# HGRN score products of a head issued by block width, both scan directions together, in place of tile by tile

## The chip, the cores and the metric

One NeuronCore of a Trainium2 chip runs the kernel. The metric is the device time of one execution in microseconds (us); three runs of the kernel before are shown, and one more execution was taken with a profile. The engines are TensorE (PE, with its weight loads as PEld), VectorE (DVE), ScalarE (ACT), GpSimd (POOL) and SyncE (SP); transfers are issued by the queues of SP and POOL.

## What is computed

The reference is a model of two layers on 256 context and 512 latent tokens of width 1024: the first layer mixes by retention and windowed attention, the second by a gated linear recurrence (HGRN) in both directions; after each comes a mixture of 32 experts. The change is in the second layer's mixer. Cut to that:

```python
def hgrn2_scan(q, k, v, log_f, s0):                 # 8 heads, dk = dv = 128, chunks of C = 16
    def step(s, inp):
        qn, kn, vn, fn = inp
        a = jnp.cumsum(fn, axis=2)
        o_inter = jnp.einsum('bhcd,bhde->bhce', qn * jnp.exp(a), s)
        diff = a[:, :, :, None, :] - a[:, :, None, :, :]
        dec = jnp.exp(jnp.where(lower, diff, NEG_INF))
        scores = jnp.einsum('bhid,bhjd,bhijd->bhij', qn, kn, dec)
        o_intra = jnp.einsum('bhij,bhje->bhie', scores, vn)
        a_last = a[:, :, -1:, :]
        s_new = jnp.exp(a_last[:, :, 0, :])[..., None] * s + jnp.einsum('bhjd,bhje->bhde', kn * jnp.exp(a_last - a), vn)
        return s_new, o_inter + o_intra
# forward and backward over the context, then over the latents from the context's final states; the two are added
```

## The kernel before

The method `odd` (L1178) runs a loop over eight heads. For each it splits the head's weights into two half-precision parts (`wsh`, `wsl`), projects all tokens (PSUM tiles `px`), and makes from them the gates `sig`, the output gate `gs` and the queries `q`; then it calls `hgrn` (L1281). The kernel works with chunks of 128 tokens in place of 16. Per head and direction d (0 forward, 1 backward) `hgrn` takes the logarithm of the gates (`lf`, L1286), their running sums (`a`, L1290 and L1291), the decayed keys `kp` (L1302) and queries `qp`, and the operands of the scores.

The scores of a tile of 128 tokens are not one product, because the exponents need a reference point near both tokens. `eq` and `ek` hold, per direction, 1024 columns: 512 with a reference in each block of 32 tokens, 256 for the off-diagonal parts of blocks of 64 (halves of 32), and 256 for those of blocks of 128 (halves of 64). The operands of the first kind are finished by L1333 and L1334, those of the two others by L1340 and L1341, eight operations in all. On PE, for each direction and each of the four latent tiles t, one full 128x128 product is written into the PSUM tile `hs`, then a 64x64 product over its off-diagonal quarter, then two 32x32 products over the smaller off-diagonal parts. Stationary operands are 128, 64 and 32 columns wide; the narrow ones stand at a column position of the array equal to the partition where their output begins. A matmul in float32 shows as two records in the trace.

When a direction's 16 products are done, VectorE applies its triangular mask (`am`, L1358). Then come the transposes of `kp` (`ktp`, L1366), their copies `kt`, the products `u`, the states `S` (L1376), and after both directions the output `ho`, its mean square `hms` and the gated output `y`. After the last head, `mix_out` multiplies `y` by the output weights (`po`), routes the tokens, and `moe` streams the experts' weights (`mw`) through rings of buffers while PE computes `pa` and `ya` (64 columns wide) and `pb` and `yb` (32 wide).

The code is written for one engine queue each; a planner of the framework puts each engine's instructions into an order of its own when the kernel is built, by their dependencies, their place in the code and its estimates of time. So work of the next head (`px`) and of the same head (`u`) stands between products that are neighbours in the code. PSUM tiles with the tag "s" (`hs`, `hms`) share two buffers; `eq`, `ek`, `a`, `qp` and the pair `lf`/`kp` have one buffer each, `sig` and `q` two.

Of the kernel before, what the change touches and what calls it, by code (L numbers as in the profile page):

```python
# [8 lines left out]
F32 = mybir.dt.float32  # L9
# [73 lines left out]
class Kern:  # L83
# [1197 lines left out]
    def hgrn(s, h, q, sg, gs, v, y, lb, wk, ps, last):  # L1281
        nc = s.nc
        V = nc.vector
        R2 = range(2)
# [26 lines left out]
        eq = wk.tile([128, 2, 1024], F32, name="eq")  # L1311
        ek = wk.tile([128, 2, 1024], F32, name="ek")
# [5 lines left out]
        for d in R2:  # L1318
# [3 lines left out]
            for i, n in enumerate((64, 128)):  # L1322
# [4 lines left out]
                c = slice(512 + 256 * i, 768 + 256 * i)  # L1327
# [7 lines left out]
        for d in R2:  # L1335
            for i, n in enumerate((64, 128)):
                hn = n // 2
                qs, ks, rr = sides(d, n)
                c = slice(512 + 256 * i, 768 + 256 * i)
                V.tensor_tensor(v3(eq[:, d, c], hn), v3(eq[:, d, c], hn), v3(q, n)[:, :, qs], op=ALU.mult)  # L1340
                V.tensor_tensor(v3(ek[:, d, c], hn), v3(ek[:, d, c], hn), v3(kl[:, d], n)[:, :, ks], op=ALU.mult)  # L1341
        ams, Ss = [], []
        for d in R2:
            sp = ps.tile([128, 512], F32, tag="s", name="hs")
            for t in range(4):
                c = slice(t * 128, (t + 1) * 128)
                s.mm(sp[:, c], ek[:, d, c], eq[:, d, c], True, True)
                c64 = slice(768 + t * 64, 832 + t * 64)
                kr, qr = (0, 64) if d == 0 else (64, 0)
                s.mm(sp[kr:kr + 64, t * 128 + qr:t * 128 + qr + 64], ek[:, d, c64], eq[:, d, c64], True, True)  # L1350
                for u in R2:
                    c32 = slice(512 + t * 64 + u * 32, 544 + t * 64 + u * 32)
                    kr, qr = (64 * u, 64 * u + 32) if d == 0 else (64 * u + 32, 64 * u)
                    nc.tensor.matmul(sp[kr:kr + 32, t * 128 + qr:t * 128 + qr + 32], ek[:, d, c32], eq[:, d, c32],
                                     start=True, stop=True, tile_position=(0, kr))
            am = wk.tile([128, 4, 128], F32, tag="am", name="am", bufs=2)
            mask = s.C["ltri" if d == 0 else "utri"]
            V.tensor_tensor(am, v3(sp, 128), mask[:, None, :].to_broadcast([128, 4, 128]), op=ALU.mult)  # L1358

            order = (0, 1, 2, 3, 4, 5) if d == 0 else (1, 0, 5, 4, 3, 2)  # L1360
            kt = wk.tile([128, 5, 128], F32, name="kt", bufs=1)
            for i0, m in ((0, 4), (4, 1)):
                tp = ps.tile([128, 512], F32, tag="t", name="ktp")
                for i in range(i0, i0 + m):
                    t = order[i]
                    nc.tensor.transpose(tp[:, (i - i0) * 128:(i - i0 + 1) * 128], kp[:, d, t * 128:(t + 1) * 128], s.ident)  # L1366
                s.copy(kt[:, i0:i0 + m], v3(tp[:, :m * 128], 128))
            S = wk.tile([128, 5, 128], F32, name="S", bufs=2)
            for i in range(5):
                t = order[i]  # L1370
                u = ps.tile([128, 512], F32, tag="t", name="u")[:, :128]
                s.mm(u, kt[:, i], v[:, t, h * 128:(h + 1) * 128], True, True)
                if i == 0:
                    V.tensor_copy(S[:, 0], u)
                else:
                    V.scalar_tensor_tensor(S[:, i], S[:, i - 1], ge[:, d, t:t + 1], u, op0=ALU.mult, op1=ALU.add)  # L1376
            ams.append(am)
            Ss.append(S)
# [3 lines left out]
        for t in range(4):  # L1382
            c = slice(t * 128, (t + 1) * 128)
# [77 lines left out]
```

## Time and profile before

| | |
|---|---|
| median of three runs | 2120.47 us (2116.13 to 2121.76) |
| the profiled execution | 2118.22 us |
| its span, first to last instruction | 2116.4 us |
| mean granted clock of PE | 0.962 |
| PE, DVE, ACT, POOL busy | 86%, 41%, 27%, 17% of the span |
| score products in the trace (`hs`) | 256 records at L144, 256 at L1354, from 1169.7 to 1485.4 us |

A share of busy time is a mean over stages that have different limits. The stretch from about 1160 to 1485 us, the loop over heads, is where the changed lines run; after 1562 us the kernel streams the second layer's experts. A full granted clock (1.00) is 2.4 GHz, 0.50 is 1.2 GHz.

### The profile page before, as it was taken

The numbers are of one execution on the slowest core, as the hardware profiler recorded it, in microseconds if no ns is written. First come the engines' busy times: TensorE is split into PE (matmuls) and PEld (weight loads), VectorE is DVE, ScalarE is ACT, GpSimd is POOL, SyncE is SP. The second block draws the span as 40 slices with busy tenths as digits, with TensorE's granted clock in tenths as the row PEclk, the third lists the DMA queues.
The fourth block names the chain that finished last, engine by engine and source line by source line (L and its number), as shares of the span: only waits on it lengthen the run. The fifth ranks groups of instructions, "written<-read, shape, count | busy, mean of one in ns | idle before, by whom it ended". The sixth has DMA issues, their size and how long they took to land. (4 is left out here: it accounts for less than half of the span.)

```text
span 2116.4 us, 26460 instructions
## 1 busy us (share of the span) xinstructions
PE 1826.7 (86%) x10109; PEld 856.4 (40%) x10109; DVE 869.3 (41%) x1823; ACT 563.1 (27%) x929; POOL 352.4 (17%) x400
## 2 busy tenths in 40 slices
PE   5999999996989999888589999999949888888872
PEld 2554444453333333233244665565523333333320
DVE  5486455686111111111555766776752112111213
ACT  4355366411111111110334435653201000000000
POOL 2000000013222232211220000000132232222213
PEclk9999999997999999999789999999969999999996
DMA  9525545484999999999853120110459999999996
GB/s 319 194 68 205 210 156 192 185 308 182 410 371 399 410 412 410 410 413 386 295 159 100 41 60 24 60 61 20 162 195 410 411 410 410 410 411 410 410 399 231
DMA packets 168717, 567.73 MB, mean 268 GB/s; under 512 B 21701, under 2 KB 69310, under 8 KB 130658
## 3 DMA queue, kind: packets, MB, share of 16 engines
q1 hardware_dynamic: 145632, 523.88, 64.2%
q0 software_dynamic: 22640, 41.30, 5.5%
q8 instruction: 127, 2.08, 0.4%
q14 instruction: 44, 0.36, 0.0%
q10 hardware_dynamic: 274, 0.10, 0.0%
HBM read 554.59 MB, written 39.91 MB: 281 GB/s over the span
## 5 line engine op out<-in xcount | busy, mean ns | idle before, releaser
L144 PE MATMUL pa<-mw,xa 128*64 128x512 f32 x2048 | 535.4, 606 | 30.6 <-DMA mw<-in_moe_w 26.5
L144 PE MATMUL ya<-mw,gT 128*64 128x512 f32 x1024 | 285.2, 602 | 2.2 <-DMA mw<-in_moe_w 1.2
L144 PEld LDWEIGHTS pa<-mw,xa 128*64 128x64 f32 x2048 | 158.0, 138 | 283.9 <-issue 276.7
L144 PE MATMUL px<-hTh,wsh 128*128 128x512 f16 (+1 forms) x672 | 225.5, 336 | 7.5 <-DVE t L438 2.8
L144 PE MATMUL px<-hTl,wsh 128*128 128x512 f16 (+1 forms) x672 | 225.5, 336 | 1.9 <-DVE hTl L348 1.8
L144 PE MATMUL px<-hTh,wsl 128*128 128x512 f16 (+1 forms) x672 | 225.4, 336 | 0.0
L144 PEld LDWEIGHTS <-wsh 128*128 128x128 f16 x1344 | 130.4, 98 | 117.4 <-issue 19.0
L1027 DVE TENSOR_TENSOR gg<-gg,pa 128x256 f32<-128x256 f32 x64 | 26.9, 420 | 333.0 <-ACT gg L1026 333.0
L937 POOL DMA_INDIRECT yd<-sb,ixm x64 | 65.9, 1029 | 581.0 <-DVE sb L1062 294.1
L144 PEld LDWEIGHTS ya<-mw,gT 128*64 128x64 f32 x1024 | 79.7, 136 | 114.3 <-issue 99.3
L1027 DVE TENSOR_TENSOR gg<-gg,pb 128x128 f32<-128x128 f32 x64 | 18.4, 288 | 253.1 <-ACT gg L1026 253.1
L1026 ACT ACTIVATE gg<-pa 128x256 f32<-128x256 f32 x64 | 24.6, 384 | 361.6 <-PE pa L144 361.6
L138 DVE SCALAR_TENSOR_TENSOR wsl<-w,wsh 128x2048 f16<-128x2048 f32 x34 | 77.8, 2290 | 35.2 <-ACT wsh L135 31.3
L1026 ACT ACTIVATE gg<-pb 128x128 f32<-128x128 f32 x64 | 17.8, 277 | 276.1 <-PE pb L144 276.1
L1032 PE MATMUL gt<-cca,gg 128*128 128x128 f32 x192 | 46.5, 306 | 50.5 <-DVE gg L1027 50.5
L144 PEld LDWEIGHTS <-wsl 128*128 128x128 f16 x672 | 65.9, 98 | 50.2 <-issue 3.9
L927 POOL DMA_INDIRECT hga<-h2d,ixm x64 | 66.7, 1042 | 103.7 <-PE xt L987 77.7
L1032 PEld LDWEIGHTS gt<-cca,gg 128*128 128x128 f32 x192 | 21.5, 141 | 147.5 <-DVE gg L1027 98.8
L144 PE MATMUL adaps<-adaw,cT 128*32 128x512 f32 x384 | 75.8, 636 | 4.2 <-DMA adaw<-in_ada_w 2.9
L937 POOL DMA_INDIRECT yd<-sa,ixm x64 | 64.2, 1004 | 69.5 <-ACT sa L1046 34.1
L992 ACT ACTIVATE xa<-xt 128x512 f32<-128x512 f32 x64 | 38.2, 597 | 140.1 <-PE xt L987 137.8
L144 PE MATMUL pv<-wsh,hTh 128*128 128x512 f16 (+1 forms) x192 | 70.0, 365 | 5.9 <-ACT hTh L1227 5.9
(391 smaller groups left out, 2810.2 us busy)
## 6 DMA issues: line engine op xcount, KB each, us to landing
mw<-in_moe_w SPq DMA_DIRECT2D x384, 1024.0 KB, 20.9
adaw<-in_ada_w SPq DMA_DIRECT2D x40, 1024.0 KB, 5.0
w<-in_od_w_in SPq DMA_DIRECT2D x32, 512.0 KB, 5.5
adaw<-in_ada_w SPq DMA_DIRECT2D x16, 512.0 KB, 7.3
w<-in_ev_w_in SPq DMA_DIRECT2D x8, 1024.0 KB, 7.1
cy<-yd SPq DMA_DIRECT2D x12, 512.0 KB, 9.5
xmid<-oxr POOLq DMA_DIRECT2D x10, 512.0 KB, 6.4
h2d<-ohp POOLq DMA_DIRECT2D x10, 512.0 KB, 3.1
```

The lines of the kernel that those rows point to most:

```text
L138: i = s.nc.vector.scalar_tensor_tensor(lo, v, WS, hi, op0=ALU.mult, op1=ALU.subtract)
L144: return s.nc.tensor.matmul(ps, lhsT, rhs, start=first, stop=last)
L927: i = nc.gpsimd.indirect_dma_start(out=hg[e % NG][g], out_offset=None, in_=hv[g], in_offset=bass.IndirectOffsetOnAxis(ap=cols[g][0], axis= ...
L937: i = nc.gpsimd.indirect_dma_start(out=yv[g], out_offset=bass.IndirectOffsetOnAxis(ap=cols[g][1], axis=0), in_=yt, in_offset=None, bounds_ ...
L992: nc.scalar.activation(x, v, AF.Copy)
L1026: nc.scalar.activation(g[:, c0:c0 + n], p[:, :n], AF.Silu)
L1027: nc.vector.tensor_tensor(g[:, c0:c0 + n], g[:, c0:c0 + n], p[:, n:2 * n], op=ALU.mult)
L1032: nc.tensor.transpose(t[:, c * 128:(c + 1) * 128], g[:, c * 128:(c + 1) * 128], s.ident)
```

## The change

The two PSUM tiles of a head are taken at once, and the 32 matmuls of its scores are issued in three runs: the eight full products, one direction after the other; then the eight 64-wide ones, tile by tile with the direction innermost; then the sixteen 32-wide ones, by tile, block and direction. The masks and all that follows come after, direction by direction as before. The matmuls, their operands and their outputs are the same ones.

```diff
         ams, Ss = [], []
+
+        sps = [ps.tile([128, 512], F32, tag="s", name="hs") for d in R2]
         for d in R2:
-            sp = ps.tile([128, 512], F32, tag="s", name="hs")
             for t in range(4):
                 c = slice(t * 128, (t + 1) * 128)
-                s.mm(sp[:, c], ek[:, d, c], eq[:, d, c], True, True)
+                s.mm(sps[d][:, c], ek[:, d, c], eq[:, d, c], True, True)
+        for t in range(4):
+            for d in R2:
                 c64 = slice(768 + t * 64, 832 + t * 64)
                 kr, qr = (0, 64) if d == 0 else (64, 0)
-                s.mm(sp[kr:kr + 64, t * 128 + qr:t * 128 + qr + 64], ek[:, d, c64], eq[:, d, c64], True, True)
-                for u in R2:
+                s.mm(sps[d][kr:kr + 64, t * 128 + qr:t * 128 + qr + 64], ek[:, d, c64], eq[:, d, c64], True, True)
+        for t in range(4):
+            for u in R2:
+                for d in R2:
                     c32 = slice(512 + t * 64 + u * 32, 544 + t * 64 + u * 32)
                     kr, qr = (64 * u, 64 * u + 32) if d == 0 else (64 * u + 32, 64 * u)
-                    nc.tensor.matmul(sp[kr:kr + 32, t * 128 + qr:t * 128 + qr + 32], ek[:, d, c32], eq[:, d, c32],
+                    nc.tensor.matmul(sps[d][kr:kr + 32, t * 128 + qr:t * 128 + qr + 32], ek[:, d, c32], eq[:, d, c32],
                                      start=True, stop=True, tile_position=(0, kr))
+        for d in R2:
+            sp = sps[d]
             am = wk.tile([128, 4, 128], F32, tag="am", name="am", bufs=2)
```

## Rows read from the trace of the kernel before

**Rows 1.** The page: PE's busy tenths and granted clock, 40 slices of the span.
```profile
PE   5999999996989999888589999999949888888872
PEclk9999999997999999999789999999969999999996
```
**Rows 2.** Stretches of a head: us, busy of each engine, clock; sum of seven.
```profile
core 0: us, PE busy (x) PEld busy (x) DVE busy (x) ACT busy (x) POOL busy (x), PEclk, DMA share, GB/s
1205.00:1244.00 39.00, 37.12 (x250) 23.96 (x250) 30.64 (x48) 18.85 (x22) 0.00 (x0) 1.00 0.30 82
...
sum 311.50, PE 297.35 PEld 186.42 DVE 219.61 ACT 153.94 POOL 1.13; mean PE 42.48 PEld 26.63 DVE 31.37 ACT 21.99 POOL 0.16
```
**Rows 3.** PE's waits, 1155 to 1470 us: us in total, times, longest.
```profile
PE ktp L1366 <- DVE kp L1302: 13.8, 8, 2.9
```
**Rows 4.** Timeline of VectorE, first head: start, us, operation, idle before and releaser.
```profile
1173.75 0.69 DVE L1358 TENSOR_TENSOR am<-hs,ccb 128x512 f32<-128x512 f32 x1 [2.00 <-PE hs L1354]
...
1177.42 0.69 DVE L1358 TENSOR_TENSOR am<-hs,ccb 128x512 f32<-128x512 f32 x1 [2.27 <-PE hs L1354]
```
**Rows 5.** Timeline of SP's queue, and a stretch (as rows 2) of the experts.
```profile
1562.65 72.10 SPq L951 DMA_DIRECT2D mw<-in_moe_w  x32
...
1700.00:1800.00 100.00, 87.90 (x405) 31.23 (x407) 19.83 (x42) 8.81 (x21) 27.50 (x27) 1.00 1.02 410
```
**Rows 6.** Timeline of PE, first head (matmul records; neighbours at one line merged).
```profile
1170.60 0.33 PE L144 MATMUL hs<-eq,ek 128*64 128x64 f32 x2
1170.86 0.26 PE L1354 MATMUL hs<-eq,ek 128*32 128x32 f32 x4
1171.05 0.75 PE L144 MATMUL hs<-eq,ek 128*128 128x128 f32 x4
1171.72 0.26 PE L1354 MATMUL hs<-eq,ek 128*32 128x32 f32 x4
...
1173.63 0.71 PE L144 MATMUL u<-ov,kt 128*128 128x128 f32 x4
...
1182.10 0.39 PE L144 MATMUL ho<-qp,S 128*128 128x128 f32 x2
1182.32 0.39 PE L144 MATMUL ho<-am,ov 128*128 128x128 f32 x2
```
**Rows 7.** Timeline of PE, experts of the first layer, narrow stationary operands.
```profile
931.80 3.74 PE L144 MATMUL pb<-mw,xb 128*32 128x256 f32 x64
935.47 0.65 PE L144 MATMUL pa<-mw,xa 128*64 128x512 f32 x2
...
975.07 1.94 PE L144 MATMUL ya<-mw,gT 128*64 128x512 f32 x8
976.94 0.44 PE L1032 MATMUL gt<-cca,gg 128*128 128x128 f32 x2
```
**Rows 8.** Timeline of PE, windows 1170.861 to 1170.866, then 1170.868 to 1170.869.
```profile
1170.86 0.22 PE L1354 MATMUL hs<-eq,ek 128*32 128x32 f32 x1
...
1170.86 0.22 PE L1354 MATMUL hs<-eq,ek 128*32 128x32 f32 x2
```
**Rows 9.** Timeline of VectorE, second head: the operands of the scores.
```profile
1211.39 1.23 DVE L1333 TENSOR_TENSOR eq<-eq,q 128x1024 f32<-128x1024 f32 x1
1212.53 0.43 DVE L1340 TENSOR_TENSOR eq<-eq,q 128x256 f32<-128x256 f32 x1
...
1214.87 0.43 DVE L1341 TENSOR_TENSOR ek<-ek,sig 128x256 f32<-128x256 f32 x1
```
**Rows 10.** The last head: a stretch (as rows 2), and the timeline of PE.
```profile
1475.70:1489.30 13.60, 13.55 (x77) 10.47 (x77) 3.81 (x10) 1.43 (x2) 0.00 (x0) 0.50 0.01 2
...
1474.01 0.71 PE L144 MATMUL hs<-eq,ek 128*128 128x128 f32 x4 [0.90 <-DVE eq L1333]
1477.31 1.20 PE L144 MATMUL hs<-eq,ek 128*128 128x128 f32 x4
1478.69 1.20 PE L144 MATMUL hs<-eq,ek 128*128 128x128 f32 x4
...
1485.33 0.80 PE L144 MATMUL ho<-am,ov 128*128 128x128 f32 x2
```

## Prediction

> **What bounds the kernel now.** I read the page first, then the stretch in which the changed lines run, then what ends last in that stretch. The page [rows 1] shows TensorE (PE) busy for 86% of the span, at full clock nearly throughout. The score products lie between about 1170 and 1485 us [rows 6, 10], in the loop over eight heads. Cut from one head's first transpose to the next, seven heads take 311.5 us, 44.5 each; PE is busy 297.4 of these, VectorE 219.6, ScalarE 153.9 [rows 2]. The waits of PE say what the rest is: 13.8 us in eight waits for `kp` (L1302), one at each head's beginning, and nothing else of size [rows 3]. So this stretch is bound by PE's instruction stream, with one short wait a head on a chain of VectorE and ScalarE. That chain starts with the Ln of L1286, which needs the next head's gates (`sig`, made from `px` that PE issues behind this head's scores) and the buffer that this head's last `ktp` frees: both are behind the scores on PE, so time taken out of the scores moves the chain too. VectorE stands still for the scores: it waits 2.00 and 2.27 us for them before the two masks of one head [rows 4].
>
> After the loop everything hangs on it: the output projection, the routing, and the experts' weights, whose steady loading begins at 1562.65 us and then runs at 410 GB/s [rows 5]. The loading starts when the routing is done, so what the loop gains moves the end by as much.
>
> **What the scores cost.** One head is shown in [rows 6]. A tile's group is a 128-wide product, a 64-wide and two 32-wide ones (each matmul is two records of the trace). From 1170.86 to 1171.72 a group takes 0.86 us. The 64-wide pair takes 0.26 of it (1170.60 to 1170.86), the four 32-wide records 0.19 (1170.86 to 1171.05), the 128-wide pair the other 0.41. Eight groups: 6.88 us a head, seven heads 48, and the last head more (below).
>
> Most of that isn't work. Products of the same 128 columns that follow each other at one width (`ho`) take 0.22 us a pair, 0.112 a record [rows 6]. By columns, 64 need 0.056 and 32 need 0.028 a record. So of the 128-wide pair 0.19 us is overhead (0.41 - 0.22), of the 64-wide pair 0.15 (0.26 - 0.11), of the 32-wide records, which run two at a time, 0.13 (0.185 - 2 x 0.028): 0.47 us a group is spent on entering and leaving widths, 3.8 us a head.
>
> **The change part by part.**
> *Widths entered.* 24 stages a head become three, so the 0.47 us is paid once. The 128-wide stage then costs 8 x 0.223 = 1.79 us.
> *The narrow stages.* The 64-wide stage has 16 records; with d innermost, neighbours go to different halves of the columns (0 and 64). The 32-wide stage has 32 records, whose neighbours go to 0, 32, 64, 96. Whether they run side by side is read from the experts: 64 records of `pb`, 32 wide with 256 columns, take 3.67 us, 0.057 each where 0.223 would be a single one's; eight of `ya`, 64 wide with 512 columns, take 1.87 us, 0.23 each against 0.45 [rows 7]. So four run together, and two. Lower bounds: 16 x 0.056 / 2 = 0.45 and 32 x 0.028 / 4 = 0.22 us. Upper bounds: no row shows records following each other for long faster than `pb`'s 0.057; at that pace they cost 0.9 and 1.8. I take the lower ones, as the pieces of the present groups already start together: two windows 6 ns apart hold one and two started 32-wide records [rows 8].
> Sum a head: 1.79 + 0.45 + 0.22 + 0.47 = 2.93 us, 3.95 less than now; by the upper bounds 4.96, 1.9 less.
> *A wait that is added.* Both directions' narrow stages now stand ahead of everything else, and alternate. The 64-wide stage needs the last of the eight products of L1340/L1341; in the second head these run from 1212.53 to 1215.3 [rows 9], while the 128-wide stage, beginning as L1333 ends at about 1212.7, ends near 1214.6. That is up to 0.8 us. Up to the last head PE has no wait for these operands that shows [rows 3], so the planner puts other work into such gaps; I charge less than half, 0.35 us. Queued behind that wait on PE are `ktp`, `u`, `ho` and the next `px`. It leaves **3.6 us a head**, 25.2 for seven.
> *The masks.* The second now runs 3.7 us behind the first [rows 4]; both will be released together, where all scores end. `ho` needs both, 1.4 us of VectorE, during which PE has `ktp`, `u` and `px`. If that cover were gone it would cost 0.7 us a head. PSUM has two buffers of this tag and both were in use before; nothing is charged. The number of matmuls, bytes and queue entries stays; SP's and POOL's queues hold nothing of it.
> *The last head* runs at half clock from 1475.7 to 1489.3 [rows 10]: its groups take 1.39 us (1477.31 to 1478.69), and scores with one `u` between stretch from 1474.01 to 1485.33. With the change: 1.9 us for the first stage, a wait for the last L1341 to about 1476.7 (2.6 us behind L1333's end, as in [rows 9]), then the two narrow stages and overhead at 1.39/0.86 of their time, (0.45 + 0.22 + 0.47) x 1.6 = 1.8: the end is near 1478.6, 6.2 us earlier once the `u` pair is left out. But if the half clock lasts as long, the `ktp`, `u` and `ho` that come behind it run at half clock for some 6 us more than now and give about half back. I take 3.5, bounds 2 and 6.2.
> *Sum.* 25.2 + 3.5 = 28.7 us. The profiled execution took 2118.2 us; it would take 2089.5. It lies 2.3 us under the median of the three runs shown (2120.47); I put the forecast between, at 2091.
>
> **The rivals.**
> *Issue is the limit.* The narrow stages go no faster than `pb`'s records: 1.9 us a head, 7 x 1.9 + 2 = 15 us, **2104**. For it: no longer run in the trace is faster. Against: [rows 8], and that `pb` is at its full fourfold rate by columns, so it shows no limit of issue. The Trainium skill, "TensorE: Matmul & The Clock Gate", section "Wait — 56ns, not 53.3ns?", says that start-to-start never drops below about 25 ns however small a matmul is. By that page the 32-wide stage would take 32 x 0.025 = 0.8 us instead of 0.22, an estimate that gives 4.6 us of the gain back: 2096. The two windows [rows 8] disagree for two records on different columns; no row shows a longer run.
> *The planner splits the stages.* It already puts `u` between two scores [rows 6]. Each product of full width inside a narrow stage costs a leaving and an entering, about 0.3 us; six a head would halve the gain: **2105**. Against: PE's other work has room before and behind.
> *The two directions don't overlap.* They write two PSUM banks, and `pb` and `ya` write one. If each change of bank cost what a change of width does, the 64-wide stage would take 8 x 0.26 = 2.1 us, the 32-wide one 16 x 0.185 = 3.0, the first 1.98: 7.1 against 6.9, nothing gained: **2121**.
> *The clock falls* (the slower side). In the last head, soon after a wait of 0.90 us ahead of the scores, PE was granted 0.50 for 13.6 us [rows 10]. Denser scores that end sooner leave PE with more waiting or narrow work in each head. A fall costs half of 13.6, 6.8 us, where PE is the bound; it decides from the fifth of seven heads on (5 x 6.8 = 34, over 28.7). All seven: 2118 - 29 + 48 = **2139** with the median's offset. Against: a wait of 2.9 us for `kp` [rows 3] leaves the clock of the seven other heads at 1.00 (one of their seven rows stands in [rows 2]).
>
> **How the numbers follow.** Forecast 0.68 (2081 to 2100); issue 0.13; split stages 0.06; no overlap 0.05; clock 0.05; something else without effect 0.03. Low end: 7 x 3.95 + 6.2 = 33.9 off 2118.2, and 3 for waits for `kp` that shift: 2081. High end: 15 off the median is 2105, plus the same 3: **2081 to 2108** also holds the issue and split cases. About 0.3%, 6.4 us, is what a measurement of this kernel tells from no change; faster by more 0.87, within 0.08, slower 0.05.
>
> **What would show it.** Right: each head's scores as one 128-wide run of 16 records, one of 64, one of 32, over in 3 to 3.6 us in place of about 7; VectorE's two masks back to back; heads of about 41 us with PE still waiting only for `kp`; the steady load of the experts 29 us earlier; the rest of the trace shifted and otherwise the same. Wrong: 32-wide records 25 or 57 ns apart (issue), `px` or `u` between narrow records (planner), 0.26 us for each 64-wide pair (banks), half clock in other heads, or PE waiting for something new and long between the scores and the next Ln.

## The result and the profile after

The changed kernel takes 2089.33 us (median, 2086.97 to 2089.85), the kernel before 2121.11 in the same measurement: a ratio of 0.9847, 95% interval 0.9828 to 0.9865. It is faster by 31.8 us where 29.5 were forecast (2120.47 to 2091), and 2089.33 lies within 2 us of the forecast. How it came there differs in three terms of the sum, which partly cancel; that is what the rest is about.

The page of the changed kernel, PE's busy tenths and granted clock in 40 slices, to be read against [rows 1]:
```profile
PE   5999999996989999888589999999959888888882
PEclk9999999998999999999889999999969999999996
```
As a whole it is the picture of before: the change isn't to be seen at this size.

The stretches of a head in the changed kernel, cut where PE's wait ahead of the head's first `ktp` begins, columns as in [rows 2]:
```profile
core 0: us, PE busy (x) PEld busy (x) DVE busy (x) ACT busy (x) POOL busy (x), PEclk, DMA share, GB/s
1158.00:1202.90 44.90, 42.64 (x290) 26.26 (x289) 31.23 (x52) 25.54 (x28) 0.00 (x0) 0.96 0.09 24
1202.90:1237.80 34.90, 33.79 (x248) 22.58 (x247) 30.92 (x50) 19.08 (x23) 0.00 (x0) 1.00 0.34 91
...
1325.60:1362.00 36.40, 33.60 (x231) 21.81 (x230) 30.48 (x52) 20.61 (x24) 0.00 (x0) 0.95 0.16 58
...
sum 288.90, PE 277.13 PEld 177.28 DVE 216.99 ACT 153.82 POOL 1.14; mean PE 39.59 PEld 25.33 DVE 31.00 ACT 21.97 POOL 0.16
```
The sum of [rows 2] starts further ahead, 2.5 us before the first `ktp`. Cut as here, the kernel before has:
```profile
sum 310.20, PE 296.93 PEld 186.36 DVE 218.31 ACT 153.54 POOL 1.13; mean PE 42.42 PEld 26.62 DVE 31.19 ACT 21.93 POOL 0.16
```
PE's busy time fell by 19.8 us, and the stretches by 21.3; VectorE, ScalarE and the number of instructions stayed. PE is still the bound, and it still waits for one thing only. PE's waits in these heads (us in total, times, longest), against [rows 3]:
```profile
PE ktp L1373 <- DVE kp L1302: 12.4, 8, 2.8
```
One head's scores before are shown in [rows 6]. PE's timeline of the first and the second head of the changed kernel (start, us, engine, line, operation, records; neighbours at one line are merged, so x32 at L144 holds 16 records of 128 columns and 16 of 64):
```profile
1171.91 2.67 PE L144 MATMUL hs<-eq,ek 128*128 128x128 f32 x32
1174.51 0.46 PE L1359 MATMUL hs<-eq,ek 128*32 128x32 f32 x32
1174.90 0.71 PE L144 MATMUL u<-ov,kt 128*128 128x128 f32 x4
...
1211.63 2.56 PE L144 MATMUL hs<-eq,ek 128*128 128x128 f32 x24
1214.12 0.31 PE L1359 MATMUL hs<-eq,ek 128*32 128x32 f32 x6
1214.36 0.68 PE L144 MATMUL hs<-eq,ek 128*64 128x64 f32 x8
1214.97 0.45 PE L1359 MATMUL hs<-eq,ek 128*32 128x32 f32 x26
1215.34 0.49 PE L144 MATMUL u<-ov,kt 128*128 128x128 f32 x2
```
In the first head the three stages are whole, as the source writes them: from 1171.91 to the start of `u` at 1174.90 they take 2.99 us. In the second the 64-wide stage is in two pieces: eight records of one direction, six 32-wide ones, eight 64-wide ones of the other direction, the other 26. That takes 3.71 us (1211.63 to 1215.34). Seven of the eight heads have this cut. VectorE's timeline in this head shows the last operands of the scores, those of the second direction's 64-wide products:
```profile
1213.35 0.43 DVE L1340 TENSOR_TENSOR eq<-eq,q 128x256 f32<-128x256 f32 x1
1213.68 0.43 DVE L1341 TENSOR_TENSOR ek<-ek,sig 128x256 f32<-128x256 f32 x1
```
They are ready at 1214.11; the 64-wide stage begins at 1213.51, with the other direction.

VectorE's masks of the first head, against [rows 4]:
```profile
1175.03 0.69 DVE L1365 TENSOR_TENSOR am<-hs,ccb 128x512 f32<-128x512 f32 x1 [1.11 <-PE hs L1359]
1175.89 0.69 DVE L1365 TENSOR_TENSOR am<-hs,ccb 128x512 f32<-128x512 f32 x1
```
They follow each other, with one wait for the scores instead of two. The last head, PE's timeline, against [rows 10]:
```profile
1447.86 0.55 PE L1373 MATMUL ktp<-cca,kp 128*128 128x128 f32 x3 [0.93 <-DVE kp L1302]
1454.10 2.66 PE L144 MATMUL hs<-eq,ek 128*128 128x128 f32 x24 [0.91 <-DVE eq L1333]
...
1458.05 0.49 PE L144 MATMUL u<-ov,kt 128*128 128x128 f32 x2
```
A stretch of it, columns as in [rows 2]:
```profile
1454.00:1460.00 6.00, 5.80 (x79) 5.22 (x79) 5.23 (x15) 0.10 (x1) 0.00 (x0) 1.00 0.00 0
```
The start of the experts' steady load on SP's queue, against [rows 5]:
```profile
1534.61 103.61 SPq L951 DMA_DIRECT2D mw<-in_moe_w  x44
```
The scores take 3.95 us (1454.10 to 1458.05) instead of 11.3, and the clock is at 1.00 where it was at 0.50. The load begins at 1534.61 instead of 1562.65: 28.0 us earlier, nearly the whole difference of the two spans (2116.4 to 2088.1).

**Where the time went.** Before, the first `ktp` of the first and of the last head start at 1159.54 and 1468.44 us, after at 1160.27 and 1447.86. The span is 28.3 us shorter: 0.7 lost ahead of the loop, 21.3 won in seven heads, 7.8 from the last head to the end. Of the 21.3, the scores won 19.7 (45.6 to 25.9), PE's idle time 1.5 (the fourth head's wait for `kp` is 1.20 us instead of 2.87), `u`, `ho` and `po` 2.5; `px` and `ktp` lost 1.9 and 0.6, as two stretches of 3.4 us at half clock now lie mostly in them (below).

The same quantities of every profiled execution; the experiments named here follow. All times in us; the scores are PE's time from the first to the last of them without other work between, and "at 0.50" counts the stretches at half clock in the eight heads (one more, of 34 to 38 us, lies around the start of the load in every execution).
```
kernel                     seven heads  last head   scores of      wait    at 0.50
                           ktp to ktp   to load     7 heads/last   for kp
before                       308.9        94.2       45.6 / 10.8    13.8   last head, 13.6
after                        287.6        86.75      25.9 / 3.95    12.4   2 x 3.4
e0 after again               287.8        86.7       25.9 / 3.95    12.4   2 x 3.4
e1 directions apart          295.2        87.2       28.8 / 4.14    15.7   3 x 3.4
e4 wide operands first       281.5        85.95      21.1 / 3.12    12.4   1 x 3.4
e6 32-wide stage first       282.3        86.0       22.1 / 3.29    12.4   1 x 3.4
e3 no alternation            289.95       87.3       25.6 / 3.60    16.0   3 x 3.4
e5 order pinned              283.5        86.1       22.1 / 3.22    14.4   1 x 3.4
e7 last head by tile         284.9        93.8       26.0 / 9.38    12.4   last head, 10.2
e8 before, wide operands     312.5        93.45      46.2 / 9.4     13.7   2 x 3.4; last head, 10.2
```
The first `ktp` starts at 1156.5 us in e3 and at 1163.3 in e0, although the source ahead of the loop is the same. A whole execution can thus differ by some us for reasons that lie ahead of the loop, so the loop's own time is given beside the medians. The experiments were measured in two groups, each beside the kernel before: e0, e1, e4 and e6 (where it took 2119.71 us), and e3, e5, e7 and e8 (2120.08). Between the groups the ratios are compared.

### The profile page after: what moved, and what is told of

It reads as the page before. It is cut to its first block, busy times and chain, and to the rows that moved or that the text cites. A ratio compares the mean times of both kernels' runs of the same rounds, so it can differ in the third digit from the quotient of the medians.

```text
span 2088.1 us, 26462 instructions
## 1 busy us (share of the span) xinstructions
PE 1802.3 (86%) x10109; PEld 843.4 (40%) x10109; DVE 869.0 (42%) x1823; ACT 563.3 (27%) x929; POOL 353.3 (17%) x400
## 5 line engine op out<-in xcount | busy, mean ns | idle before, releaser
L144 PE MATMUL pa<-mw,xa 128*64 128x512 f32 x2048 | 537.0, 608 | 28.9 <-DMA mw<-in_moe_w 24.6
L144 PE MATMUL ya<-mw,gT 128*64 128x512 f32 x1024 | 283.8, 602 | 2.3 <-DMA mw<-in_moe_w 1.5
L144 PEld LDWEIGHTS pa<-mw,xa 128*64 128x64 f32 x2048 | 158.4, 139 | 284.1 <-issue 277.4
L144 PE MATMUL px<-hTh,wsh 128*128 128x512 f16 (+1 forms) x672 | 227.1, 339 | 7.5 <-DVE t L438 2.8
L144 PE MATMUL px<-hTl,wsh 128*128 128x512 f16 (+1 forms) x672 | 227.3, 338 | 2.7 <-DVE hTl L348 2.6
L144 PE MATMUL px<-hTh,wsl 128*128 128x512 f16 (+1 forms) x672 | 226.9, 338 | 0.0
L144 PEld LDWEIGHTS <-wsh 128*128 128x128 f16 x1344 | 131.2, 98 | 118.9 <-issue 22.8
L144 PEld LDWEIGHTS ya<-mw,gT 128*64 128x64 f32 x1024 | 79.3, 136 | 114.4 <-issue 98.3
L144 PEld LDWEIGHTS <-wsl 128*128 128x128 f16 x672 | 66.3, 99 | 51.4 <-issue 6.0
L144 PE MATMUL adaps<-adaw,cT 128*32 128x512 f32 x384 | 75.7, 633 | 4.5 <-DMA adaw<-in_ada_w 3.4
L144 PE MATMUL pv<-wsh,hTh 128*128 128x512 f16 (+1 forms) x192 | 69.0, 360 | 5.8 <-ACT hTh L1227 5.8
```

The costliest lines, as they stand in the source:

```text
L144: return s.nc.tensor.matmul(ps, lhsT, rhs, start=first, stop=last)
```

## The experiments

The theory: a head's scores cost their columns at full rate, plus a price for each width that is entered, and the planner cuts the stage whose operands are late. The rivals were the prediction's: the records' issue, the split, the PSUM banks, the clock. In the diffs, `p128(d, t)`, `p64(d, t)` and `p32(d, t, u)` stand for the three matmul calls of the changed kernel.

**e0: the changed kernel again**, beside the others.

> The changed kernel itself, timed beside the others so that they can be set against it on one chip: 2089 us, 28 to 32 us under the kernel before. Its last head tells whether the full clock there is the kernel's or an accident of one execution: if the kernel's, the trace shows the last head's scores in about 4.0 us at clock 1.00 again; if an accident, they take 6 us or more at 0.50.

Measured 2090.68 us (2088.22 to 2093.31), ratio 0.9858 [0.9843, 0.9873]. The result repeats, with the same cut in the same heads (25.9 us of scores in seven heads), and the last head's scores again take 3.95 us at full clock.

**e1: the two directions one after the other**, each by width.
```diff
-        for d in R2:
-            for t in range(4): p128(d, t)
-        for t in range(4):
-            for d in R2: p64(d, t)
-        for t in range(4):
-            for u in R2:
-                for d in R2: p32(d, t, u)
+        for d in R2:
+            for t in range(4): p128(d, t)
+            for t in range(4): p64(d, t)
+            for t in range(4):
+                for u in R2: p32(d, t, u)
```

> By width, but each direction by itself: six stages a head, and no direction next to the other. If the gain comes from widths that are entered less often (theory), a head's scores take 2 x (4 x 0.223 + 0.19, 8 x 0.056 + 0.15, 16 x 0.028 / 2 + 0.13) = 4.1 us against 3.8 in the changed kernel, so 2 to 4 us are lost: 2091 to 2093. If it comes from the two directions running side by side (rival), most of it goes: 2105 or more.

Measured 2100.05 us (2095.23 to 2103.51), ratio 0.9905 [0.9891, 0.9919]. PE's timeline of its first head:
```profile
1170.31 1.77 PE L144 MATMUL hs<-eq,ek 128*128 128x128 f32 x16
1172.00 0.45 PE L1358 MATMUL hs<-eq,ek 128*32 128x32 f32 x16
1172.38 1.77 PE L144 MATMUL hs<-eq,ek 128*128 128x128 f32 x16
1174.08 0.45 PE L1358 MATMUL hs<-eq,ek 128*32 128x32 f32 x16
1174.45 0.38 PE L144 MATMUL u<-ov,kt 128*128 128x128 f32 x1
```
The scores take 4.14 us, as the theory's price of six entered widths wants; but the kernel is some 9 us slower than e0, not the 2 to 4 that were expected. The loop of the profiled execution shows 7.4 of it (295.2 against 287.8): 2.8 in the scores, 3.3 more of waiting for `kp` (15.7 against 12.4), and about 1.5 for one more stretch at half clock. So the expected time was missed though the expected cost of the scores was met.

The longer wait lies in two heads: the fourth, 2.87 us against 1.20 in e0, and the seventh, 2.87 against 1.03. VectorE's timeline ahead of the fourth head, first of the changed kernel, then of e1:
```profile
1280.39 1.22 DVE L1309 TENSOR_TENSOR qp<-qp,q 128x1024 f32<-128x1024 f32 x1
1281.52 1.75 DVE L1302 TENSOR_TENSOR kp<-kp,sig 128x1536 f32<-128x1536 f32 x1
...
1281.60 1.22 DVE L1309 TENSOR_TENSOR qp<-qp,q 128x1024 f32<-128x1024 f32 x1
1282.74 0.42 DVE L1329 TENSOR_TENSOR ek<-a 128x256 f32<-128x256 f32 x1
...
1283.74 1.76 DVE L1302 TENSOR_TENSOR kp<-kp,sig 128x1536 f32<-128x1536 f32 x1
```
In e1 the planner put three short operations on the scores' exponents (L1329, L1328, L1329) ahead of the last one on `kp` (L1302). That one starts 1.4 us behind the end of ScalarE's step before it (1282.34) instead of 0.2 (1281.33). The kernel before has the same order, and the same 2.87 us, in its fourth head. So the longer wait is an order on VectorE, for which the theory has no term. Why the planner chose it isn't shown, nor where the 2 us lie by which the medians differ beyond the loop.

**e4: VectorE makes the 64-wide stage's operands first**, for both directions.
```diff
-        for d in R2:
-            for i, n in enumerate((64, 128)):
+        for i, n in ((1, 128), (0, 64)):
+            for d in R2:
```

> The changed kernel with VectorE's eight products of L1340/L1341 in another order: both directions' operands of the 64-wide products first, then those of the 32-wide ones. In seven heads of the changed kernel the 64-wide stage is cut in two (one direction, some 32-wide products, the other direction). If the planner cuts it because the second direction's operands come late (theory), it is whole here, four and four run side by side, and a head's scores take 3.0 us in place of 3.8: 5 to 6 us faster than the changed kernel, 2084. If the cut has another cause, or PE only waits longer (rival), no difference: 2089.

Measured 2082.11 us (2080.49 to 2084.35), ratio 0.9821 [0.9807, 0.9834]: faster than the changed kernel, and its interval lies apart from that of e0, measured beside it. PE's timeline of its second head and of its last:
```profile
1210.27 2.56 PE L144 MATMUL hs<-eq,ek 128*128 128x128 f32 x32
1212.76 0.49 PE L1358 MATMUL hs<-eq,ek 128*32 128x32 f32 x32
1213.18 0.49 PE L144 MATMUL u<-ov,kt 128*128 128x128 f32 x2
...
1446.59 2.67 PE L144 MATMUL hs<-eq,ek 128*128 128x128 f32 x32 [0.90 <-DVE eq L1333]
```
The cut is gone in every head: 2.91 us here, 21.1 in seven heads against 25.9. So it was the late operands that cut the stage, and the cut cost the changed kernel about 0.8 us in each head that has it. Of the 8.6 us between the medians of e0 and e4 the trace shows 5.6 in the scores (4.8 in seven heads, 0.8 in the last); e4's loop also has one stretch at half clock less. This is the fastest of the versions here.

**e6: the 32-wide stage ahead of the 64-wide one**, with the operands of the 32-wide stage made first (`for i, n in ((0, 64), (1, 128))` outside, `for d in R2` inside).

> The changed kernel with the 32-wide stage ahead of the 64-wide one, and VectorE's operands of the 32-wide products first. Theory as for the run with the 64-wide operands first: whole stages, 3.0 us of PE a head; but the 64-wide stage then waits for VectorE's last product (2.7 us behind the start of the scores, where the two stages before end at 2.4), 0.3 us a head: 4 us faster than the changed kernel, 2085. Rival: order and cuts make no difference, 2089.

Measured 2087.26 us (2082.28 to 2089.99), ratio 0.9844 [0.9831, 0.9858]. Its scores (22.1) and its loop (282.3) are close to e4's; its median lies 2 us above the expected one, its runs are wider, and by the intervals it can be told neither from e0 nor from e4. PE's timeline of its third head:
```profile
1247.70 0.99 PE L144 MATMUL hs<-eq,ek 128*64 128x64 f32 x16
1248.62 0.49 PE L144 MATMUL u<-ov,kt 128*128 128x128 f32 x2
```
The stage is whole but takes 0.92 us, where e4's takes 0.61, as in six of the eight heads it begins with one direction alone: the other's first record starts at 1248.01, just behind VectorE's last operand (1247.96). So in either order whole stages bring the loop near e4's, and a late operand can take the alternation from a stage without cutting it.

**e3: e4 without alternation.** Same stages and operands as e4, neighbours on the same columns.
```diff
-        for t in range(4):
-            for d in R2: p64(d, t)
-        for t in range(4):
-            for u in R2:
-                for d in R2: p32(d, t, u)
+        for d in R2:
+            for t in range(4): p64(d, t)
+        for d in R2:
+            for u in R2:
+                for t in range(4): p32(d, t, u)
```

> The kernel with the 64-wide operands first, three whole stages a head, but inside the narrow stages neighbours go to the same columns (directions one after the other, and the 32-wide ones of one column position in a row of four). If products on different columns run side by side and those on the same columns one by one (theory), the 64-wide stage takes 16 x 0.056 + 0.15 = 1.05 us in place of 0.6, the 32-wide one 32 x 0.028 + 0.13 = 1.03 in place of 0.37: 4.1 us a head in place of 3.0, 8 to 9 us slower than with alternation, 2091. If only the number of stages counts (rival), no difference: 2082.

Measured 2090.43 us (2088.82 to 2092.09), ratio 0.9865 [0.9849, 0.9882]: 8.3 us above e4 by the medians, 9.3 by the ratios. PE's timeline of its first head, the 64-wide stage again by itself from a narrower window:
```profile
1168.11 2.95 PE L144 MATMUL hs<-eq,ek 128*128 128x128 f32 x32
...
1170.09 0.97 PE L144 MATMUL hs<-eq,ek 128*64 128x64 f32 x16
...
1170.98 0.90 PE L1358 MATMUL hs<-eq,ek 128*32 128x32 f32 x32
1171.81 0.38 PE L144 MATMUL u<-ov,kt 128*128 128x128 f32 x1
```
The 64-wide stage takes 0.89 us (1170.09 to 1170.98) where e4's takes 0.61, the 32-wide one 0.83 instead of 0.4 to 0.5. The alternation is worth 0.64 us a head; I had expected 1.05 and 1.03 for the stages. They cost less because runs on different columns overlap where they meet. The records of the 64-wide stage start 58 ns apart; by this spacing the second run begins at 1170.376, 6 ns behind the fifth of the first run's eight records, and the two go side by side to 1170.545. The 64-wide stage changes columns once, the 32-wide one three times. Of the loop's 8.5 us the scores are 4.5; the wait for `kp`, 16.0 us in e3 and 12.4 in e4, is 3.6 more. It grew in two heads again, the fourth (2.87 us, with the order on VectorE that e1 has there) and the last (3.09 against 0.93). e5 below, which alternates, has the 3.09 in its last head too, so it isn't alternation as such that sets this wait.

**e5: the changed kernel with the narrow stages pinned**: `p64` and `p32` each wrapped in the framework's call that keeps an instruction at its place in the program, operands in the old order.

> The changed kernel with the narrow products held in the order of the code, so that the planner can't cut the 64-wide stage; VectorE's order is the changed kernel's. The second 64-wide product then waits for the second direction's operands, and the planner may fill with other work behind the first one. Theory: one more entering and leaving and a wait of some tenths of a us a head, 3.3 us in place of 3.8: 2086. If waiting costs what the cut costs (the price of 0.8 us a head that the prediction half charged): 2090.

Measured 2085.5 us (2083.78 to 2089.48), ratio 0.9846 [0.9829, 0.9863]. A later head, PE's timeline:
```profile
1245.03 2.31 PE L144 MATMUL hs<-eq,ek 128*128 128x128 f32 x18
1247.27 0.39 PE L144 MATMUL px<-hTh,wsl 128*128 128x512 f16 x1
...
1248.02 0.68 PE L144 MATMUL hs<-eq,ek 128*64 128x64 f32 x14
1248.63 0.46 PE L1358 MATMUL hs<-eq,ek 128*32 128x32 f32 x32
1249.02 0.71 PE L144 MATMUL u<-ov,kt 128*128 128x128 f32 x4
```
This is the picture that the prediction had drawn: the wait for the second direction's operands is filled with `px`. Only the first 64-wide product (two records) stands ahead of it; the other seven and the 32-wide stage are whole (22.1 us in seven heads). The loop is 4.3 us shorter than e0's. By the medians' intervals it can't be told from the changed kernel; the loop's time is what speaks for it.

**e7: the last head by tile.** The changed kernel in seven heads; under `if h == 7:` the loops of before (`d`, `t`, then `p128`, `p64`, two `p32`).

> The changed kernel with the last head's scores tile by tile, as before the change. If the order of the scores is what made the clock fall in the last head (theory), it falls there again to 0.50 for some 13 us, the last head takes 7 to 8 us longer and the time is 2097. If the clock has nothing to do with the order (rival), only the widths entered are lost, 3 us: 2093.

Measured 2094.44 us (2091.16 to 2096.8), ratio 0.9877 [0.986, 0.9893], between the two expected times, and its interval overlaps e0's. The trace is clearer. PE's timeline in the last head:
```profile
1454.03 0.71 PE L144 MATMUL hs<-eq,ek 128*128 128x128 f32 x4 [0.91 <-DVE eq L1333]
1455.46 0.30 PE L144 MATMUL hs<-eq,ek 128*64 128x64 f32 x2 [0.72 <-DVE ek L1341]
1459.25 1.20 PE L144 MATMUL hs<-eq,ek 128*128 128x128 f32 x4
```
Two stretches of it, columns as in [rows 2]:
```profile
1453.00:1457.00 4.00, 2.38 (x22) 1.75 (x20) 3.92 (x10) 0.66 (x1) 0.00 (x0) 1.00 0.00 0
1458.30:1468.40 10.10, 9.62 (x54) 7.70 (x53) 2.74 (x7) 1.60 (x2) 0.00 (x0) 0.50 0.00 1
```
The half clock is back, for 10 us, and the last head takes 93.8 us to the load, 7.1 more than e0's. By tile, PE waits for VectorE, starts a group, and waits again for the next operand (0.72 us): 2.38 us of work in the first 4. Then it runs its groups without a wait, 2.69 us of work in the 2.75 up to the fall at 1458.15. By width it has 16 wide records to run during the second wait (5.80 of 6.00 busy in the changed kernel's stretch above). So the last head's gain hangs on how its scores are ordered; whether the second wait or the groups behind it bring the fall isn't shown. The whole profiled execution is only 3.5 us longer than e0's, because its seven heads, without a stretch at half clock, are 2.9 us shorter.

**e8: the kernel before with e4's order of VectorE's operands**, nothing else.

> The kernel before with VectorE's eight products in the order of the run with the 64-wide operands first, and nothing else. Theory: that order helps only where whole stages wait for both directions; tile by tile it changes nothing, 2120 within 3 us. Rival: the order of VectorE's work is a gain of its own, 5 us or more: 2114.

Measured 2123.57 us (2118.99 to 2128.15), ratio 1.0015 [1.0003, 1.0027]. That is 3.5 us above the kernel before as measured beside it (2120.08 us), just outside the expected 3, and to the slow side. The operands' order alone gains nothing: it only helps stages that want one kind of operand from both directions.

## Why the prediction was right

**The bound and the end: right.** The loop got shorter by what PE got shorter, and the load of the experts moved by as much as the loop and the last head. The 311.5 us for seven heads starts ahead of the first `ktp`; from there it is 308.9, 44.1 a head. No term of the sum rests on it.

**What the scores cost: too high.** I took 6.88 us a head from one group of 0.86. Seven heads measure 45.6, 6.5 a head: 0.37 too much. One group was read where the whole head stood in the trace.

**The stages: right.** Where they are whole (first head) the 128-wide stage takes 1.98 us, as 1.79 + 0.19; the 64-wide 0.615 for 0.45 + 0.15; the 32-wide 0.39 for 0.22 + 0.13. Together 2.98 against 2.93. The lower bounds, taken for the narrow stages against `pb`'s pace, were the true ones, and e3 shows what they rest on: the alternation of columns.

**"A wait that is added": the step that failed.** I saw that the 64-wide stage's last operands come late, and supposed that the planner would fill that gap with other work, for 0.35 us. It filled it with 32-wide scores instead, which cuts the 64-wide stage into its two directions. Then the 64-wide products no longer alternate, so each half costs 0.61 us, as much as the whole did (2 x 0.61 - 0.615 = 0.6), and the two pieces of the 32-wide stage take 0.62 to 0.75 us together instead of 0.39. The scores came to 3.70 us a head, where 2.93 and the 0.35 make 3.28. With the base, 0.37 + 0.42 of the 3.6 us were not there: 2.8 remain, 19.7 in seven heads; PE's other work and its waits, which the sum doesn't have, added 1.6 to make 21.3; most of that is the fourth head's wait for `kp`, by the planner's order on VectorE. e4 took the cause away (the late operands) and got the stages whole.

**The last head: half of what it was worth.** I gave back half of 6.2 us because the half clock would last as long as before. There was none; the last head gave 7.5 us up to the load and 7.8 to the end, not 3.5. Missed by 3.9 below in seven heads (21.3 for 25.2) and by 4.3 above in the last, the sum of 28.7 met 28.3 by compensation. That the forecast lies so near is luck; that the narrow stages run side by side, and that widths are paid for once a run, isn't.

**The masks, the queues: right at nothing.** The masks run back to back, as shown above against [rows 4], and PE had `u` to do.

**The rivals.** *Issue:* fell. In e4's first head, a window of 30 ns holds four started 32-wide records and one that ends 0.21 us later holds 30:
```profile
1173.13 0.24 PE L1358 MATMUL hs<-eq,ek 128*32 128x32 f32 x4
...
1173.13 0.45 PE L1358 MATMUL hs<-eq,ek 128*32 128x32 f32 x30
```
That is 8 ns from start to start, as the two windows of [rows 8] suggested. The floor of about 25 ns that the Trainium skill states ("TensorE: Matmul & The Clock Gate", section "Wait — 56ns, not 53.3ns?") doesn't hold for neighbours on different columns here; e3's 32-wide records on the same columns start 32 ns apart, which is in keeping with it. *Banks:* fell; a 64-wide stage that alternates between two banks takes 0.615 us, not 2.1. *Split stages:* happened, in another form than feared: scores between scores, not full-width work, at about 0.8 us in a head. *Clock:* a fall to 0.50 did come, in the loop's heads too, but for 3.4 us at a time and in up to three heads of an execution:
```profile
1161.20:1164.60 3.40, 3.40 (x11) 1.46 (x9) 3.40 (x10) 1.39 (x2) 0.00 (x0) 0.50 0.00 0
...
1328.50:1331.80 3.30, 3.30 (x12) 2.23 (x13) 3.16 (x8) 2.26 (x3) 0.00 (x0) 0.50 0.00 0
```
These are the changed kernel's two (columns as in [rows 2]), both just behind a wait for `kp` at a head's beginning; they don't stand at the scores. They cost about 1.5 us each, most of it in `px`: e7's seven heads, in much the same order and without one, take 2.9 us less than e0's with two.

## What to carry to other kernels

Here matmuls of several widths cost 0.13 to 0.19 us for each run of one width, on top of the columns in it: gather them by width, let neighbours of a narrow width go to different columns, and count the runs. Then look at the order in which the operands are made: here the planner cut the stage whose operands were late, and moving the producers (e4, 2082.11 us, ratio 0.9821, against 0.9858 for the change alone) brought 8.6 us that the reordering had left, 5.6 of them in the scores. And a step's cost is read from the whole of it in the trace, not from one piece times eight.

## What the runs showed of the hardware

- 32-wide fp32 records on four column positions start 8 ns apart (26 in 0.21 us, e4), on the same columns 32 ns apart (e3). Changing the columns at one width cost nothing: the next columns' first record started 5 to 6 ns behind the fifth of the eight records before it (e3). Entering a width cost 0.13 to 0.19 us. The Trainium skill, "TensorEngine Tiling (Array Packing)", section "Key Properties", says that a change of tiling mode drains the engine and a change of tile doesn't. The traces agree in the times, and give the price; the drain itself can't be seen in them.
- In the last head, which has no `px` of a next head to fill waits, the clock was granted at 0.50 during the scores in all three executions whose last head runs by tile (13.6, 10.2 and 10.2 us: before, e7, e8) and in none of the seven that run it by width. Before it fell, PE had waited two or three times for VectorE at the head of the scores (0.9 and 0.7 us before and in e7; 0.9, 0.3 and 0.3 in e8) and had then run groups by tile, for 0.2 us in the kernel before, 2.7 in e7 and 2.3 in e8. At half clock a group took 1.39 us [rows 10].
- Stretches of 3.4 us at 0.50 come and go between kernels whose loops hardly differ (0 to 3 of them in the table). All 15 begin at the end of a wait for `kp` of 2.2 to 3.1 us or within 1.6 us behind it; 12 other waits as long have none behind them. What decides between them isn't shown.
